# First layer's projections: bias columns copied on ScalarE, the last values' buffer placed apart from the accumulators, the second layer's gate sums spread later

## The chip, the cores and the metric

The kernel runs on one core of one Trainium2 chip. The metric is device time in microseconds (us), taken from the start to the end of one execution on that core. The engines of the core are named as the profile names them: PE is the matrix engine (PEld its weight loads), DVE is VectorE, ACT is ScalarE, POOL is GpSimd, SP issues most transfers (SPq is its queue). Each engine works through its own instructions in order and waits at an instruction until what it needs is there.

## The reference, cut to what matters

Two layers run over 256 context tokens and 1024 latent tokens of width 1024. The first layer is a windowed attention, the second a latent attention. Both start with a normalisation whose scale and shift come from a conditioning vector; a gate from the same vector weighs the layer's output.

```python
def adaln(cond, w, bias):
    m = jax.nn.silu(cond) @ w + bias
    return jnp.split(m, 3, axis=-1)          # shift, scale, gate
...
    hx = rms_norm(x, norm_g[i]) * (1.0 + scale_x[:, None]) + shift_x[:, None]
    hc = rms_norm(ctx, norm_g[i]) * (1.0 + scale_c) + shift_c
...
    q, k, v, g = jnp.split(h @ w_in, [A_WIDTH, A_WIDTH + A_KV_WIDTH, A_WIDTH + 2 * A_KV_WIDTH], axis=-1)
...
    x = x + gate_x[:, None] * yx
```

All values are float32. The conditioning product (a vector of 1024 by a 1024 x 3072 matrix, for two conditioning vectors and two layers) is the part called "sums" below; `h @ w_in` with its 2560 output columns is the part called "projections".

## The kernel before, in words

A float32 product is made of three matmuls, one line each (L126, L127, L128 in the helper `mm3`): both operands are split into a rounded high part and a rest, and high x high, low x high and high x low are added in one PSUM bank. The helper `split` makes the two parts: L121 casts the high part on ACT, L122 subtracts it on POOL or DVE.

The first layer's input projection is cut into ten blocks of 256 columns (`blocks`; number 0 is the values, 1, 6, 8 and 9 are gates, 7 is the keys, the others are queries). A block's weights come in four pieces of two 128-row chunks each (`Pieces`), loaded into float32 staging and cast into one of two weight buffers. A projection (`proj_t`, written below as block/group/half) takes one half of a block (128 columns) and one group of tokens: group 0 is the 256 context tokens, groups 1 and 2 are 512 latent tokens each. It consists of 24 matmuls into one of six PSUM banks that are used in turn (banks 0 to 5). The shift of the normalisation isn't added to the tokens: two more columns (256 and 257 of group 0) carry it through the same matmuls, so that the product's columns 256 and 257 are the bias of that half block, and are copied out of PSUM (L489). `post_t` empties the bank with that bias: L501 on ACT for a gate block (the result is stored by L502 on SP), L532 on ACT and L533 on DVE for queries of group 0, L507 on ACT followed by L508, L514, L529 on DVE (the rotation) for queries of groups 1 and 2, with stores L537 on SP.

The values (block 0) are computed first, without the shift, into five buffers `Vraw`, one per 256 tokens. Their bias comes later (`v_bias`): L446 and L455 on PE, L459 on DVE adds it to each of the five buffers, and `split` casts them (L121 on ACT, L122 on POOL).

The conditioning sums that the first attention doesn't need at once are worked off in small steps between the projections (`ada_rest`): a group is 512 of the 3072 columns, and each of its eight 128-row chunks is multiplied by a conditioning scalar and added to an accumulator on DVE (L191 the first chunk, L193 the others). A group has two accumulators (one per conditioning vector), the last two groups only one. After a group's last chunk PE sums over the partitions (L203, or L220 for a gate group), and DVE adds the bias (L211, or L221 for a gate). `ada_run(n)` takes n of these steps. The accumulators `acc1` lie at 30 and 32 KB of the float arena, the second of them also holds the small copy `mtmp` of `v_bias` until L455 has read it; a fifth `Vraw` buffer lies at 30 KB too.

All this is written as a program in order, but a scheduler places the instructions on each engine, by the data they need and its own estimates of when things are ready; what lies in one buffer is kept in order by waits. So an edit moves instructions on several engines, and their new order is shown below.

Of the kernel before, what the change touches and what calls it, by code (L numbers as in the profile page):

```python
# [34 lines left out]
class Ring:  # L35
# [6 lines left out]
    def next(self):  # L42
        b = self.bufs[self.i % len(self.bufs)]
        self.i += 1
        return b


def shp(ap, *dims):
    n = 1
    for d in dims:  # L50
        n *= d
    ap = ap[:, 0:n]
    if len(dims) == 1:
        return ap
    names = "abcdefg"[: len(dims)]
    kw = {c: d for c, d in zip(names[1:], dims[1:])}
    return ap.rearrange("p (" + " ".join(names) + ") -> p " + " ".join(names), **kw)
# [3 lines left out]
def kernel(ctx: ExitStack, tc: tile.TileContext, t, out, dbg=None):  # L61
    nc = tc.nc
# [23 lines left out]
    def r_at(kb, *dims):  # L86
        n = int(np.prod(dims))
        return shp(R[:, int(kb * KB) : int(kb * KB) + n], *dims)

    def f_at(kb, *dims):  # L90
        n = int(np.prod(dims))
        return shp(F[:, int(kb * KB) : int(kb * KB) + n], *dims)
# [31 lines left out]
    def mm3(o, a, b, first, last):  # L124
        (ah, al), (bh, bl) = a, b
        nc.tensor.matmul(o, ah, bh, start=first, stop=False)  # L126
        nc.tensor.matmul(o, al, bh, start=False, stop=False)  # L127
        nc.tensor.matmul(o, ah, bl, start=False, stop=last)  # L128
# [170 lines left out]
    wst = [80 + Z, 96 + Z]  # L299
    kT = r_at(112 + Z, 4, TOK)  # L300
    V = r_at(132 + Z, NT, 4, 128)
    Vraw = [f_at(o, 2, 256) for o in (0, 2, 10, 12, 30)]
    cosa = f_at(0, SEQ)
    sina = f_at(10, SEQ)
    stg = Ring(F, [4, 6, 8], 512)
# [76 lines left out]
    def ada_run(n):  # L382
        for _ in range(n):
            next(ada, None)
# [86 lines left out]
    bias = {}  # L471

    def proj_t(bi, gp, c):

        W = wt[bi]
        ps = pss()
        if gp:
            o = shp(ps, 2, 256)
            m = [hw[gp][:, :, s] for s in range(2)]
        else:  # L480
            o = ps[:, 0:258]
            m = [hT[0][:, s] for s in range(2)]
        cs = slice(c * 128, c * 128 + 128)
        for k in range(8):
            b = [x[:, :, k, :] if gp else x[:, k, :] for x in m]
            mm3(o, [W[:, s, k, cs] for s in range(2)], b, k == 0, k == 7)
        if gp == 0:
            bias[bi, c] = biases()
            nc.vector.tensor_copy(bias[bi, c], ps[:, 256:258])  # L489
        return ps  # L490

    def post_t(bi, gp, c, ps):
# [335 lines left out]
    for i, (gp, c) in enumerate([(1, 0), (1, 1), (2, 0), (2, 1)]):  # L828
        held.append((1, gp, c, proj_t(1, gp, c)))
        if i == 0:  # L830
            ada0.cols(0, 0, acc0[0], pst())
        if i == 1:
            ada0.cols(0, 1, acc0[1], pst())
            nc.scalar.copy(hT[0][:, 0, :, 256:258], ada0.B)
            nc.vector.tensor_sub(hT[0][:, 1, :, 256:258], ada0.B, hT[0][:, 0, :, 256:258].bitcast(F32))
            nc.vector.tensor_copy(B32[:, :, 0:2], ada0.B)
            vb = v_bias()
        if i == 2:
            next(vb)
        if i == 3:  # L840
            next(vb)
            load(out=cosa, in_=t["cos_a"])
            load(out=sina, in_=t["sin_a"])
            ada = ada_rest()
    for c in range(2):
        ps = proj_t(1, 0, c)
        for x in held[c::2]:
            post_t(*x)
        post_t(1, 0, c, ps)
        for _ in range(2):  # L850
            pieces.cast()
            pieces.load()
    for bi in range(2, 8):
        for i, (gp, c) in enumerate([(0, 0), (0, 1), (1, 0), (1, 1), (2, 0), (2, 1)]):
            post_t(bi, gp, c, proj_t(bi, gp, c))
            if bi < 7:
                ada_run(4 if gp == 0 else 6 if bi == 6 else 2)
            if 1 <= i < 5:
                pieces.cast()
                pieces.load()  # L860
    for bi in (8, 9):
        for c in range(2):
            ps = proj_t(bi, 0, c)
            if bi == 8:
                pieces.cast()
                pieces.load()
                pieces.cast()
            post_t(bi, 0, c, ps)
            ada_run(4)
    for gp in (1, 2):  # L870
        for bi in (8, 9):
            for c in range(2):
                if (bi, gp, c) == (8, 2, 0):
                    load2(out=mask, in_=t["mask"])
                    load2(out=gx, in_=gate_d[0, 0, :].partition_broadcast(128))
                    load2(out=gc, in_=gate_d[0, 1, :].partition_broadcast(128))
                    units[0].prep_q()
                    units[0].prep()
                    units[1].prep_q()
                if (bi, gp, c) == (9, 2, 0):  # L880
                    units[1].prep()
                    units[2].prep_q()
                    for h in range(4):
                        units[0].score(h)
                post_t(bi, gp, c, proj_t(bi, gp, c))
                ada_run(1)
                for _ in range(2 if gp == 2 else bi - 8):
                    next(wo_fill, None)

# [817 lines left out]
```

## Time and profile before

| | us |
|---|---|
| median of 3 runs | 1592.23 (1592.12 to 1593.79) |
| profiled execution, its own time | 1592.02 |
| its span | 1590.2 |
| PE busy in the span | 1544.0 |
| DVE, ACT, POOL busy | 994.1, 771.3, 750.1 |

The difference of 1.8 us between the profiled execution's time and its span lies around the span. The projections of the first layer run from about 95 to 355 us of the span. In most stages the matmuls follow each other without a gap, and so the time is read best from the few places where PE waits. A matmul's start to the next one's start is 0.12 us for 258 columns and 0.23 us for 512 at full clock.

### The profile page before, as it was taken

How to read it: one execution, taken by the hardware profiler on the slowest of the kernel's cores; microseconds unless marked ns; L12 is line 12 of the kernel's file. 1: busy time of each engine (PE TensorE's matmuls, PEld its weight loads, DVE VectorE, ACT ScalarE, POOL GpSimd, SP SyncE). 2: the span in 40 equal slices, each digit the busy share in tenths (PEclk: the TensorE clock that was granted, in tenths of full speed). 3: DMA queues.
4: the chain of work that ended last, by engine and by line, in shares of the span. 5: the costliest groups of instructions: out<-in, count | busy, mean ns of one | idle time of the engine just before them, and what ended most of it. 6: DMA issues, size and time to landing. Idle time of an engine off the chain costs nothing.

```text
span 1590.2 us, 26835 instructions
## 1 busy us (share of the span) xinstructions
PE 1544.0 (97%) x9830; PEld 1228.2 (77%) x9830; DVE 994.1 (63%) x1773; ACT 771.3 (49%) x1468; POOL 750.1 (47%) x805
## 2 busy tenths in 40 slices
PE   7989999998999999998999999999999999999998
PEld 3878888786878888887998899766766766766687
DVE  2867997827867777778525302666667566567354
ACT  3522222248767777767413332455555555545322
POOL 1241121125665444454214250488688688689410
PEclk8999999999999999999999999999999999999999
DMA  7456665544343333337103753313232323244251
GB/s 250 157 155 186 202 199 186 179 137 119 98 126 93 94 91 91 92 99 219 37 31 114 264 175 94 103 31 103 68 96 81 84 80 103 61 136 111 68 166 67
DMA packets 147204, 192.81 MB, mean 121 GB/s; under 512 B 13937, under 2 KB 84081, under 8 KB 147073
## 3 DMA queue, kind: packets, MB, share of 16 engines
q1 hardware_dynamic: 145456, 188.94, 40.0%
q10 hardware_dynamic: 1616, 2.17, 0.5%
q8 instruction: 77, 1.26, 0.3%
q14 instruction: 55, 0.44, 0.1%
HBM read 144.90 MB, written 46.15 MB: 120 GB/s over the span
## 4 chain that ended last, share of the span: by engine, by line
PE 84%; DVE 4%; POOL 4%; issue 3%; ACT 3%; DMA 2%; SPq 0%; POOLq 0%; ACTq 0%; DVEq 0%
PE PB L126 14%; PE PB L127 14%; PE PB L128 14%; PE PB L1334 11%; PE PB L1356 8%; PE PB L1297 4%; PE PB L616 4%; PE PB L657 4%; PE PB L647 4%; PE PB L1305 1%; DVE arena_f L193 1%; PE PB L1385 1%; ACT arena_r L121 1%; DVE arena_r L122 1%; POOL arena_r L122 1%
## 5 line engine op out<-in xcount | busy, mean ns | idle before, releaser
L126 PE MATMUL PB<-arena_r 128*128 128x512 f32 (+3 forms) x1496 | 509.6, 342 | 12.0 <-ACT arena_f L501 5.4
L127 PE MATMUL PB<-arena_r 128*128 128x512 f32 (+3 forms) x1496 | 503.6, 337 | 2.6 <-POOL arena_r L684 0.8
L128 PE MATMUL PB<-arena_r 128*128 128x512 f32 (+3 forms) x1496 | 502.0, 336 | 0.0
L1348 POOL TENSOR_TENSOR arena_f<-arena_f 128x512 f32<-128x512 f32 x252 | 325.0, 1290 | 79.4 <-ACT arena_f L1340 62.6
L126 PEld LDWEIGHTS PB<-arena_r 128*128 128x128 f32 x1496 | 285.1, 191 | 49.6 <-ACT arena_f L501 5.6
L127 PEld LDWEIGHTS PB<-arena_r 128*128 128x128 f32 x1496 | 286.3, 191 | 30.3 <-DVE arena_r L122 1.9
L128 PEld LDWEIGHTS PB<-arena_r 128*128 128x128 f32 x1496 | 286.2, 191 | 29.2 <-issue 1.7
L122 POOL TENSOR_TENSOR arena_r<-arena_f,arena_r 128x512 fp32r<-128x512 f32 x88 | 119.5, 1372 | 291.2 <-ACT arena_r L121 240.6
L1340 ACT ACTIVATE arena_f<-PB 128x1024 f32<-128x1024 f32 x160 | 164.3, 1027 | 108.4 <-PE PB L1334 68.4
L1299 DVE TENSOR_REDUCE arena_f<-PB 128x1 f32<-128x1024 f32 x128 | 156.0, 1219 | 86.6 <-PE PB L1297 86.5
L1334 PE MATMUL PB<-arena_r 64*128 64x512 f32 (+1 forms) x1600 | 202.2, 392 | 0.3 <-ACT arena_f L1340 0.3
L1334 PEld LDWEIGHTS PB<-arena_r 64*128 64x128 f32 (+1 forms) x1600 | 146.0, 185 | 31.5 <-ACT arena_f L1340 1.8
L122 DVE TENSOR_TENSOR arena_r<-PB,arena_r 128x512 fp32r<-128x512 f32 (+1 forms) x186 | 124.1, 674 | 62.2 <-ACT arena_r L121 61.2
L1356 PE MATMUL PB<-arena_f 128*64 128x512 f32 x640 | 144.4, 597 | 0.0
L627 DVE CUSTOM_DVE_ANT_0 arena_f<-PB,arena_f,small 128x640 f32<-128x640 f32 (+2 forms) x176 | 125.2, 722 | 19.5 <-PE PB L616 12.8
L630 ACT ACTIVATE arena_f<-arena_f,small 128x640 f32<-128x640 f32 (+2 forms) x160 | 119.5, 747 | 35.1 <-DVE small L627 32.5
L121 ACT CAST arena_r<-PB 128x512 fp32r<-128x512 f32 (+1 forms) x186 | 105.3, 573 | 46.9 <-PE PB L647 44.2
L121 ACT CAST arena_r<-arena_f 128x512 fp32r<-128x512 f32 (+3 forms) x141 | 83.7, 602 | 75.8 <-PE PB L127 11.8
L657 PE MATMUL PB<-arena_r 128*128 128x512 f32 x336 | 115.7, 428 | 0.5 <-DVE arena_f L669 0.4
L616 PE MATMUL PB<-arena_r 128*128 128x256 f32 (+1 forms) x576 | 111.0, 308 | 1.6 <-DVE small L627 1.3
L1356 PEld LDWEIGHTS PB<-arena_f 128*64 128x64 f32 x640 | 43.1, 136 | 83.2 <-issue 79.9
L647 PE MATMUL PB<-ident,arena_f 128*128 128x128 f32 x672 | 103.9, 274 | 1.3 <-DVE arena_r L122 1.1
(179 smaller groups left out, 1930.5 us busy)
## 6 DMA issues: line engine op xcount, KB each, us to landing
arena_f<-ada_w SPq DMA_DIRECT2D x47, 512.0 KB, 4.5
arena_r<-q_d SPq DMA_DIRECT2D x80, 256.0 KB, 4.1
arena_r<-qn_d SPq DMA_DIRECT2D x64, 256.0 KB, 3.8
arena_r<-qr_d SPq DMA_DIRECT2D x192, 64.0 KB, 3.2
arena_f<-a_w_in SPq DMA_DIRECT2D x40, 256.0 KB, 3.4
arena_f<-x SPq DMA_DIRECT2D x16, 512.0 KB, 4.4
g_d<-arena_f SPq DMA_DIRECT2D x32, 256.0 KB, 3.3
q_d<-arena_f SPq DMA_DIRECT2D x64, 128.0 KB, 2.7
```

The lines of the kernel that those rows point to most:

```text
L121: nc.scalar.copy(hi, src)
L122: (lo_eng or nc.vector).tensor_sub(lo, src, hi.bitcast(F32))
L126: nc.tensor.matmul(o, ah, bh, start=first, stop=False)
L127: nc.tensor.matmul(o, al, bh, start=False, stop=False)
L128: nc.tensor.matmul(o, ah, bl, start=False, stop=last)
L616: nc.tensor.matmul(S[:, at : at + n], qT[:, s, hq, :], kT[:, g, k : k + n], start=s == 0, stop=s == 1)
L647: nc.tensor.transpose(pt[:, h, :], self.Ps[h][:, ci * 128 : ci * 128 + 128], ident)
L657: nc.tensor.matmul(self.pv, V[:, self.chunks[ci], self.g, :], PT[:, s], start=ci == 0 and s == 0, stop=ci == self.m - 1 and s == 1,)
L1334: nc.tensor.matmul(S[:, t], k[r, c : c + 128], q[r], start=j == 0, stop=j == 4)
L1340: nc.scalar.activation(E, self.S, AF.Exp)
L1348: eng.tensor_add(self.acc, self.acc, E[:, t])
L1356: nc.tensor.matmul(self.pv[p : p + 64], Vq[:, cs[t], self.h % 4, :], E[:, t], start=i == 0, stop=i == 4)
```

## The change

Three edits, and what they do to the order of the instructions:

1. The two bias columns of each context projection are copied out of PSUM by ACT instead of DVE (18 instructions L489).
2. The fifth `Vraw` buffer moves from 30 KB to 34 KB of the float arena. At 34 KB lies also the first buffer of the ring `qst`, in which the queries of block 2 are prepared, and one buffer of the input ring `xr`.
3. The steps of the sums are spread otherwise in blocks 8 and 9: two instead of four after each context projection, three instead of one after each projection of group 1, none after group 2. The last 17 steps, the second layer's two gate groups, are the ones that move.

```diff
-    Vraw = [f_at(o, 2, 256) for o in (0, 2, 10, 12, 30)]
+    Vraw = [f_at(o, 2, 256) for o in (0, 2, 10, 12, 34)]
...
         if gp == 0:
             bias[bi, c] = biases()
-            nc.vector.tensor_copy(bias[bi, c], ps[:, 256:258])
+            nc.scalar.copy(bias[bi, c], ps[:, 256:258])
         return ps
...
             post_t(bi, 0, c, ps)
-            ada_run(4)
+            ada_run(2)
...
                 post_t(bi, gp, c, proj_t(bi, gp, c))
-                ada_run(1)
+                ada_run(3 if gp == 1 else 0)
```

**DVE where the values get their bias.** Before (L459 is the values' bias, L489 the copies of block 1's bias columns, L191 and L193 the first group of sums):

```order
L459 TENSOR_TENSOR arena_f<-arena_f,PB 128x512 [waits PE_49]
L459 TENSOR_TENSOR arena_f<-arena_f,PB 128x512 x4
L489 COPY small<-PB 128x2 [waits PE_49]
L191 TENSOR_SCALAR arena_f<-arena_f,small 128x512 [waits DMAHW3_49,Activation_49]
L193 SCALAR_TENSOR_TENSOR arena_f<-arena_f,small 128x512 [waits DVE_49]
L191 TENSOR_SCALAR arena_f<-arena_f,small 128x512 [waits Pool_49]
L193 SCALAR_TENSOR_TENSOR arena_f<-arena_f,small 128x512 [waits DMAHW4_49,DVE_49]
L193 SCALAR_TENSOR_TENSOR arena_f<-arena_f,small 128x512 [waits DVE_49]
L489 COPY small<-PB 128x2 [waits PE_49]
```

The second L191 waits for POOL, and the copy of the bias of projection 1/0/1 stands three sums behind it. With the change, at the same place:

```order
L836 COPY arena_f<-small 128x8x2
L193 SCALAR_TENSOR_TENSOR arena_f<-arena_f,small 128x512 [waits DMAHW4_49,DVE_49]
L193 SCALAR_TENSOR_TENSOR arena_f<-arena_f,small 128x512 [waits DVE_49]
L193 SCALAR_TENSOR_TENSOR arena_f<-arena_f,small 128x512 [waits DMAHW5_49,DVE_49]
L193 SCALAR_TENSOR_TENSOR arena_f<-arena_f,small 128x512 [waits DVE_49]
L193 SCALAR_TENSOR_TENSOR arena_f<-arena_f,small 128x512 [waits DMAHW6_49,DVE_49]
L193 SCALAR_TENSOR_TENSOR arena_f<-arena_f,small 128x512 [waits DVE_49]
L459 TENSOR_TENSOR arena_f<-arena_f,PB 128x512 [waits PE_49]
L459 TENSOR_TENSOR arena_f<-arena_f,PB 128x512 x4
L191 TENSOR_SCALAR arena_f<-arena_f,small 128x512 [waits Activation_49]
L193 SCALAR_TENSOR_TENSOR arena_f<-arena_f,small 128x512 [waits DVE_49] x7
L533 SCALAR_TENSOR_TENSOR arena_f<-PB,small,arena_f 128x256 [waits PE_49,Activation_49] x2
```

The copies and the wait for POOL are gone from DVE here. One accumulator's eight sums stand ahead of L459 (its first two just ahead of L836), the other's eight behind it.

**ACT at the same place.** Before (the first rows are the values' casts, L501 empties the banks of block 1):

```order
L121 CAST arena_r<-arena_f 128x8x64 [waits DVE_49] x4
L121 CAST arena_r<-arena_f 128x8x64 [waits DVE_49,Activation_49]
L501 ACTIVATE arena_f<-PB,small 128x512 [waits DVE_49]
L501 ACTIVATE arena_f<-PB,small 128x512
L501 ACTIVATE arena_f<-PB,small 128x256 [waits PE_49]
L121 CAST arena_r<-arena_f 128x512 [waits DMAHW1_49,PE_49,Pool_49]
L121 CAST arena_r<-arena_f 128x512 [waits DMAHW2_49,PE_49,Pool_49]
L121 CAST arena_r<-arena_f 128x512 [waits DMAHW3_49,PE_49,Pool_49]
L501 ACTIVATE arena_f<-PB,small 128x512 [waits DVE_49]
```

The last row is the one that empties bank 1 (projection 1/1/1); it waits for DVE's copy. With the change:

```order
L121 CAST arena_r<-arena_f 128x8x64 [waits DVE_49] x4
L489 COPY small<-PB 128x2 [waits PE_49]
L121 CAST arena_r<-arena_f 128x8x64 [waits DVE_49]
L501 ACTIVATE arena_f<-PB,small 128x512 [waits Activation_49]
L501 ACTIVATE arena_f<-PB,small 128x512
L501 ACTIVATE arena_f<-PB,small 128x256
L121 CAST arena_r<-arena_f 128x512 [waits DMAHW1_49,PE_49,Pool_49]
L489 COPY small<-PB 128x2 [waits PE_49]
L121 CAST arena_r<-arena_f 128x512 [waits DMAHW2_49,Pool_49]
L501 ACTIVATE arena_f<-PB,small 128x512 [waits Activation_49]
L121 CAST arena_r<-arena_f 128x512 [waits DMAHW3_49,Pool_49]
L501 ACTIVATE arena_f<-PB,small 128x512 [waits DMAHW6_49]
```

The tenth row empties bank 1 now: two copies have come in ahead of it, one piece's cast has gone behind it, and it waits for nothing outside ACT. Behind these rows, the first L532 of block 2 has taken over the wait for POOL (its buffer is the one at 34 KB).

**PE at the end of the sums.** Before (L220 is the partition sum of the second layer's first gate group; 128x258 rows are projection 9/0/1, the 128x512 rows 8/1/0):

```order
L127 MATMUL PB<-arena_r 128x258
L220 MATMUL PB<-arena_f,small 2x512 [waits DVE_49]
L128 MATMUL PB<-arena_r 128x258
L126 MATMUL PB<-arena_r 128x258
L127 MATMUL PB<-arena_r 128x258
L128 MATMUL PB<-arena_r 128x258
L126 MATMUL PB<-arena_r 128x512
L127 MATMUL PB<-arena_r 128x512
```

It stands four matmuls ahead of the end of projection 9/0/1. With the change:

```order
L126 MATMUL PB<-arena_r 128x512
L127 MATMUL PB<-arena_r 128x512
L128 MATMUL PB<-arena_r 128x512
L220 MATMUL PB<-arena_f,small 2x512 [waits DVE_49]
L126 MATMUL PB<-arena_r 128x512
L127 MATMUL PB<-arena_r 128x512
```

It stands behind the whole of projection 8/1/0 now, 28 matmuls later; the second gate group's L220 goes from behind 30 of the 48 matmuls of 8/1/0 and 8/1/1 to behind projection 9/1/0, 48 matmuls after the first one.

## The prediction

> **What bounds the kernel now.** I read the page first: PE is busy for nearly the whole span, and it carries most of the chain that ended last. So the time changes where PE waits or runs slowly, and hardly elsewhere.
>
> ```profile
> PE 1544.0 (97%) x9830; PEld 1228.2 (77%) x9830; DVE 994.1 (63%) x1773; ACT 771.3 (49%) x1468; POOL 750.1 (47%) x805
> PE 84%; DVE 4%; POOL 4%; issue 3%; ACT 3%; DMA 2%; SPq 0%; POOLq 0%; ACTq 0%; DVEq 0%
> ```
>
> Next the waits of PE alone, from 100 to 345 us, where all three edits lie (engine, line, whom it waited for: total, times, longest):
>
> ```profile
> PE PB L126 <- ACT arena_f L501: 5.4, 1, 5.4
> PE PB L220 <- DVE arena_f L193: 2.4, 2, 2.1
> ```
>
> There are only these three stops. The stage view shows what each costs, as PE busy (instructions), DVE, ACT, POOL and the granted clock:
>
> ```profile
> 100.35:109.87 9.52, 9.52 (x76) 9.21 (x75) 6.15 (x9) 6.11 (x11) 7.29 (x7) 1.00 0.37 103
> 109.87:115.29 5.42, 0.01 (x2) 0.00 (x1) 5.42 (x6) 0.74 (x2) 4.03 (x3) 0.80 0.56 206
> 115.29:120.00 4.71, 4.71 (x22) 4.71 (x23) 4.38 (x8) 1.36 (x3) 0.00 (x0) 0.51 0.73 227
> 120.00:283.00 163.00, 163.00 (x849) 138.08 (x849) 137.32 (x228) 43.43 (x75) 30.88 (x21) 1.00 0.63 187
> 302.30:304.50 2.20, 0.09 (x2) 0.03 (x2) 2.08 (x4) 0.98 (x2) 0.00 (x0) 0.94 0.92 322
> 304.50:307.50 3.00, 3.00 (x7) 1.29 (x8) 1.07 (x2) 0.18 (x1) 0.00 (x0) 0.50 1.06 398
> ```
>
> After both longer stops PE runs at half clock for a while (0.51, 0.50). In between it never stops in 163 us.
>
> The first stop, in order of time (start, duration, engine, line):
>
> ```profile
> 101.25 3.08 DVE L459 TENSOR_TENSOR arena_f<-arena_f,PB 128x512 f32<-128x512 f32 x5 [8.80 <-PE PB L455]
> 101.97 3.07 ACT L121 CAST arena_r<-arena_f 128x512 fp32r<-128x512 f32 x5 [2.90 <-DVE arena_f L459]
> 102.67 11.23 POOL L122 TENSOR_TENSOR arena_r<-arena_f,arena_r 128x512 fp32r<-128x512 f32 x8 [2.23 <-ACT arena_r L121]
> 104.94 1.63 ACT L501 ACTIVATE arena_f<-PB,small 128x512 f32<-128x512 f32 x3
> 106.45 1.66 ACT L121 CAST arena_r<-arena_f 128x512 fp32r<-128x512 f32 x3
> 109.59 0.28 PE L128 MATMUL PB<-arena_r 128*128 128x258 f32 x1
> 109.64 1.47 DVE L191 TENSOR_SCALAR arena_f<-arena_f,small 128x512 f32<-128x512 f32 x1 [2.44 <-POOL arena_r L122]
> 111.03 3.41 DVE L193 SCALAR_TENSOR_TENSOR arena_f<-arena_f,small 128x512 f32<-128x512 f32 x2
> 114.37 0.15 DVE L489 COPY small<-PB 128x2 f32<-128x2 f32 x1
> 114.55 1.63 ACT L501 ACTIVATE arena_f<-PB,small 128x512 f32<-128x512 f32 x3 [6.43 <-DVE small L489]
> 115.29 0.58 PE L126 MATMUL PB<-arena_r 128*128 128x258 f32 x1 [5.41 <-ACT arena_f L501]
> ```
>
> Read it upwards. PE wants bank 1 for projection 2/0/1; L501 on ACT must empty it, and lacks a bias that L489 copies on DVE in 0.15 us; DVE is kept by sums, the first of which (L191) waited 2.44 us for POOL's last read of the fifth value buffer.
>
> The second stop:
>
> ```profile
> 302.08 0.28 PE L127 MATMUL PB<-arena_r 128*128 128x258 f32 x1
> 304.47 1.87 PE L220 MATMUL PB<-arena_f,small 128*2 128x512 f32 x2 [2.11 <-DVE arena_f L193]
> 306.26 0.58 PE L128 MATMUL PB<-arena_r 128*128 128x258 f32 x1
> 307.70 0.39 PE L127 MATMUL PB<-arena_r 128*128 128x512 f32 x1
> 314.71 1.02 PE L220 MATMUL PB<-arena_f,small 128*2 128x512 f32 x2 [0.24 <-DVE arena_f L193]
> 315.66 0.50 PE L126 MATMUL PB<-arena_r 128*128 128x512 f32 x1
> ```
>
> PE reaches the gate's partition sum before DVE's last two L193 are done:
>
> ```profile
> 302.88 1.54 DVE L193 SCALAR_TENSOR_TENSOR arena_f<-arena_f,small 128x512 f32<-128x512 f32 x2
> ```
>
> **The change, part by part.** *First stop.* The buffer at 34 KB removes the wait of L191 for POOL, and the copy on ACT takes L489 from behind the sums. Either alone would take most of the stop; together nothing of DVE stands between PE and bank 1. What ACT must now do before it empties bank 1: five value casts, three L501, two piece casts and two copies. From 101.97 the five casts, three L501 and three casts before ended at 106.45 + 1.66 = 108.11. One cast fewer (0.55) and two copies more follow. The trace has no copy of two columns on ACT; the nearest row above is L532's 256 columns, the nearest below a cast of 16 columns:
>
> ```profile
> L532 ACT ACTIVATE arena_f<-PB,small 128x256 fp32r<-128x256 f32 x8 | 3.8, 474 | 13.4 <-DVE small L489 10.5 <-DMA q_d<-arena_f 2.9
> L834 ACT CAST arena_r<-small x1: 207/207/207, 92.0 to 92.0; 128x16 fp32r<-128x16 f32 x1
> ```
>
> Between 0.21 and 0.47 us each; I take 0.21, since two columns are nearer to 16 than to 256. Bank 1 is then free at 108.11 - 0.55 + 0.42 + 0.65 (an L501 of 512 columns; 1.63 is two of them and one of 256) = 108.6, at worst 109.2. PE wants it at 109.71 (the last start, 109.59, and 0.12, which a matmul of 258 columns takes from start to start: 9.52 us for 76). So the stop is gone, by a margin of 0.5 to 1.1 us. Its worth: 115.29 - 109.71 = 5.58 us, and the half clock behind it: 22 instructions in 4.71 us that take 22 x 0.12 = 2.64 at full clock, 2.07. Together 7.65 us.
>
> All 18 copies cost ACT 3.8 us (8.5 at the upper price), hidden in a stretch where ACT is busy 43 of 163 us and PE waits for nobody, with six banks between them. Without that cover the 3.8 us would be on the path.
>
> The wait for POOL isn't deleted but goes to the first L532 of block 2, with L501 of 1/0/1, the next copies and L507 of 2/1/0 queued behind it. POOL's fifth value subtraction ended by 109.64, when L191 was let go; L532 comes later than that in any case, so it costs nothing. What is late next on ACT is L501 of 1/2/1: it takes the first store's buffer again.
>
> ```profile
> 108.38 0.34 SPq L843 DMA_DIRECT2D arena_f<-sin_a  x1
> 108.84 6.74 SPq L502 DMA_DIRECT2D g_d<-arena_f  x4
> g_d<-arena_f SPq DMA_DIRECT2D x4, 256.0 KB, 4.7
> ```
>
> The stores stand on SP behind the rotation table, which itself waits for POOL's fourth value read; the first is issued at 108.84 and lands 4.7 us later, 113.5. ACT then empties bank 3 by 114.3. PE wants bank 3 at 109.71 + 2.9 (projection 2/0/1) + 5.4 (2/1/0) = 118.0: 3.7 us to spare.
>
> DVE's sums move into its idle 8.80 us ahead of L459, against POOL's pieces there, and a sum beside POOL takes up to 1.75 us instead of 0.75:
>
> ```profile
> 91.83 0.17 DVE L211 TENSOR_TENSOR small<-PB,small 128x8 f32<-128x8 f32 x1 [3.65 <-PE PB L203]
> L193 DVE SCALAR_TENSOR_TENSOR arena_f<-arena_f,small x19: 744/750/1745, 84.7 to 123.0; 128x512 f32<-128x512 f32 x19
> 94.39 3.78 POOL L122 TENSOR_TENSOR arena_r<-arena_f,arena_r 128x512 fp32r<-128x512 f32 x3 [33.48 <-PE PB L446]
> 99.14 1.29 POOL L122 TENSOR_TENSOR arena_r<-arena_f,arena_r 128x512 fp32r<-128x512 f32 x1 [0.98 <-ACT arena_r L121]
> ```
>
> L211 at 91.83, one sum and two small instructions of about 0.2 us come first, then six sums from about 93.1: two before POOL starts, then one per 1.7 us until 98.2, one in POOL's pause, the last by 100.8 at the latest. L459 isn't held up (101.25). The page "SBUF — State Buffer" of the Trainium skill, section "Who interferes with whom", says that a DVE instruction with two SBUF inputs and a GpSimd one lock each other out for a whole instruction; the trace agrees (1745 ns against 750), and this speaks against the new place of the sums.
>
> *Second stop.* L220 stands 28 matmuls later. DVE's chain there loses three copies and stays as it is; relative to PE it ends where it ended, at 304.4 on the old clock, while PE without the stop would arrive at 302.20 (302.08 and 0.12) + 0.48 + 24 x 0.223 = 308.0 (0.223 for 512 columns: 25.00 us for 112 in the stage from 316 to 341 below). The second gate group can start on DVE only after L221, then takes L191 and seven L193. At the 0.77 of an L193 (1.54 for two) for all nine that is 6.9 us, and PE has 48 x 0.223 = 10.7 us of other matmuls. Both stops go, with about 4 us to spare. Worth: 304.47 - 302.20 = 2.27; the pair of L220 1.79 from start to start against 0.95 for the second pair (315.66 - 314.71) or less, 0.84; then 306.26 to 307.70, 1.44 for five matmuls that take 0.71, 0.73; and the 0.24 of the second pair. Together 4.1 us.
>
> The half clock after a stop of only 2.1 us is seen here. The page "TensorE: Matmul & The Clock Gate" of the Trainium skill, section "Why this matters for your kernels", has the clock fall only after pauses over about 3 us. By that rule this stop would be worth 2.5 instead of 4.1 and the sum would be 10.2; the granted clock of 0.50 decides against it.
>
> *Downstream.* PE works without a stop to the end of the projections, so all of it arrives there:
>
> ```profile
> 316.00:341.00 25.00, 25.00 (x112) 20.70 (x111) 3.21 (x5) 7.53 (x12) 5.20 (x4) 1.00 0.42 133
> 341.00:360.00 19.00, 19.00 (x107) 16.36 (x105) 8.76 (x37) 13.03 (x24) 4.65 (x7) 1.00 0.60 176
> 360.00:400.00 40.00, 35.79 (x210) 27.55 (x209) 31.59 (x93) 33.28 (x94) 23.31 (x43) 1.00 0.40 107
> ```
>
> The attention's beginning (360 to 400) is a mix of PE, ACT and DVE with DMA at 0.40, each started by PE's results, so it should move as a whole.
>
> **Sum:** 7.65 + 4.1 = 11.7 us. The profiled execution, 1592.02, becomes 1580.3; the median shown is 0.2 above it: 1580.5.
>
> **The rivals.**
>
> *A, one stop returns.* The new orders have margins of 0.5 to 1.1 us at bank 1. If six sums at 1.75 us all collide with POOL, they end at 93.1 + 10.5 = 103.6, L459 is 2.3 us late, bank 1 is free at 110.9 and PE stops for 1.2 us, with up to 2.1 us of half clock behind it: gain 8.4, time 1583.8. If instead the second stop returns whole, the gain is 7.65 and the time 1584.6. Against: POOL works 5 of these 8 us only, and the margins at L220 are 4 us. Chance 0.17.
>
> *B, the gain is given back.* PE comes 11.7 us earlier to the first attention scores, and what they need (weights of the output projection, stored queries) is set by transfers. Then the time stays at about 1592. For: PE is idle 4.2 us of 360 to 400. Against: DMA at 0.40 there, and the loads are issued when PE has freed their buffers, so they move too. Chance 0.07.
>
> *C, slower.* ACT's queue, in which L501 of 1/2/1 now waits for the first store's landing with the copies behind it, becomes what PE waits for at bank 3. It costs PE from a landing at 117.3 on, one for one and 2.1 more for the clock; from 18 us after the issue (11.7 - 2.1 = 9.6 us beyond 117.3) the kernel is slower than before, at 20 us by some 1.9 us, at 25 us by 7 (1599). Against: 4.7 us measured. With whatever else turns all of it round, chance 0.04.
>
> **How the numbers follow.** The forecast has 0.72, A 0.17, B 0.07, C 0.04. A measurement of this kernel tells about 0.2% (3.2 us) from no change, so forecast and A count as faster: 0.89; B is no change, C slower. The forecast's own bounds: the copies' price moves nothing while the margin holds; the half clock may end earlier or start elsewhere (2 us either way), so 1578 at the low end. The high end takes in A and part of a return downstream: 1587.
>
> **What would show it right or wrong.** Right: no stop of PE at L126 near 110 us; granted clock 1.00 from 100 to 300; both L220 pairs without idle time ahead of them; the first scores (L616) some 11.7 us earlier; the rest of the trace the same, moved. Wrong: L126 waiting again for L501 near 110 or at 118 (A, C); L459 starting later than 101.5 (A); the scores early but the end not (B).

## The result, and the profile after

| | before | after |
|---|---|---|
| median of 6 runs, us | 1592.17 (1591.27 to 1593.79) | 1582.12 (1581.13 to 1583.18) |
| profiled execution, us | 1592.02 | 1581.13 |
| its span, us | 1590.2 | 1579.3 |

The ratio is 0.9936 (95% interval 0.9924 to 0.9949): 10.05 us less by the medians, 10.9 by the two profiled executions. The prediction had 11.7 less and the time 1580.5, with a range of 1578 to 1587.

The waits of PE in the changed kernel, in the window that holds all three edits (80 to 345 us; engine, line, whom it waited for: total, times, longest). One short stop is left, and it is neither of the two that were forecast to go:

```profile
PE PB L203 <- DVE arena_f L193: 0.3, 1, 0.3
```

The stage view of the changed kernel (PE, PEld, DVE, ACT, POOL busy, then the granted clock, the DMA share and GB/s):

```profile
100.00:120.00 20.00, 20.00 (x135) 18.57 (x134) 17.32 (x16) 9.91 (x22) 15.10 (x10) 1.00 0.61 191
120.00:283.00 163.00, 162.59 (x844) 137.34 (x843) 136.88 (x218) 45.54 (x88) 33.46 (x23) 1.00 0.64 185
302.00:340.00 38.00, 38.00 (x170) 29.74 (x169) 13.18 (x30) 13.24 (x25) 6.63 (x7) 1.00 0.65 190
```

PE is busy for the whole of 100 to 120 and of 302 to 340, at a granted clock of 1.00, where it stood still for 5.4 and 2.4 us before. In between 0.41 us of 163 is missing, which it wasn't before.

The place of the first stop in the changed kernel, in order of time:

```profile
94.10 7.43 DVE L193 SCALAR_TENSOR_TENSOR arena_f<-arena_f,small 128x512 f32<-128x512 f32 x6
102.61 3.08 DVE L459 TENSOR_TENSOR arena_f<-arena_f,PB 128x512 f32<-128x512 f32 x5 [1.08 <-PE PB L455]
105.65 0.15 ACT L489 COPY small<-PB 128x2 f32<-128x2 f32 x1
105.72 0.62 ACT L121 CAST arena_r<-arena_f 128x512 fp32r<-128x512 f32 x1
106.90 10.96 DVE L193 SCALAR_TENSOR_TENSOR arena_f<-arena_f,small 128x512 f32<-128x512 f32 x7
108.38 0.16 ACT L489 COPY small<-PB 128x2 f32<-128x2 f32 x1
108.97 0.69 ACT L501 ACTIVATE arena_f<-PB,small 128x512 f32<-128x512 f32 x1
114.98 0.69 ACT L501 ACTIVATE arena_f<-PB,small 128x512 f32<-128x512 f32 x1 [4.82 <-DMA g_d<-arena_f]
```

DVE's six sums end at 101.53, ahead of L459, which waits for PE alone (1.08 us). Its next seven sums take 10.96 us beside POOL, 1.57 each instead of 0.75, but nobody's bias stands behind them: the copy is on ACT, and L501 empties bank 1 from 108.97 to 109.66. L501 of projection 1/2/1 waits 4.82 us for the first store to land and ends at 115.67, as it was forecast to.

The place of the second stop in the changed kernel, on DVE:

```profile
293.23 6.55 DVE L193 SCALAR_TENSOR_TENSOR arena_f<-arena_f,small 128x512 f32<-128x512 f32 x7
303.79 0.68 DVE L221 TENSOR_TENSOR arena_f<-PB,arena_f 2x512 f32<-2x512 f32 x1 [3.40 <-PE PB L220]
304.89 5.48 DVE L193 SCALAR_TENSOR_TENSOR arena_f<-arena_f,small 128x512 f32<-128x512 f32 x7
315.84 0.68 DVE L221 TENSOR_TENSOR arena_f<-PB,arena_f 2x512 f32<-2x512 f32 x1 [5.47 <-PE PB L220]
```

The roles are exchanged: it is now DVE that waits for PE's sums (3.40 and 5.47 us), where PE waited for DVE.

For where the time went, the view of two lines by their first and last start: L455 (ahead of the first edit's effect) and L616 (the first attention scores, behind the last one). Before:

```profile
L455 PE MATMUL PB<-arena_f,small x4: 377/378/379, 100.2 to 100.8; 128*128 128x256 f32 x4
L616 PE MATMUL PB<-arena_r x576: 274/283/425, 341.6 to 698.9; 128*128 128x256 f32 x130, 128*128 128x384 f32 x62
```

and after:

```profile
L455 PE MATMUL PB<-arena_f,small x4: 378/378/379, 101.5 to 102.2; 128*128 128x256 f32 x4
L616 PE MATMUL PB<-arena_r x576: 274/283/425, 332.2 to 689.5; 128*128 128x256 f32 x130, 128*128 128x384 f32 x62
```

From L455 to L616 it is 241.4 us before and 230.7 after: 10.7 us gained in the stage that the edits touch. Ahead of it 1.3 us is lost (101.5 against 100.2), behind it 1.5 is gained (1248.6 against 1247.1 us to the end of the span): together the 10.9 us of the spans. Whether the 1.3 and 1.5 belong to the change is one of the questions of the runs below.

### The profile page after: what moved, and what is told of

Read it like the earlier page. It is cut to its first block, busy times and chain, and to the rows that moved or that the text cites. A ratio compares the mean times of both kernels' runs of the same rounds, so it can differ in the third digit from the quotient of the medians.

```text
span 1579.3 us, 26829 instructions
## 1 busy us (share of the span) xinstructions
PE 1542.5 (98%) x9830; PEld 1227.4 (78%) x9830; DVE 998.0 (63%) x1755; ACT 772.2 (49%) x1486; POOL 751.9 (48%) x805
## 4 chain that ended last, share of the span: by engine, by line
PE 73%; DVE 7%; issue 4%; POOL 3%; ACT 2%; DMA 2%; SPq 0%; ACTq 0%; DVEq 0%; POOLq 0%
PE PB L1334 12%; PE PB L126 11%; PE PB L127 11%; PE PB L128 11%; PE PB L1356 9%; PE PB L1297 4%; PE PB L616 4%; PE PB L657 4%; PE PB L647 4%; DVE arena_f L193 2%; DVE arena_f L514 1%; PE PB L1305 1%; ACT arena_r L121 1%; PE PB L1385 1%; PE PB L676 1%
## 5 line engine op out<-in xcount | busy, mean ns | idle before, releaser
L616 PE MATMUL PB<-arena_r 128*128 128x256 f32 (+1 forms) x576 | 111.1, 308 | 1.5 <-DVE small L627 1.3
```

The source lines that it names most:

```text
L616: nc.tensor.matmul(S[:, at : at + n], qT[:, s, hq, :], kT[:, g, k : k + n], start=s == 0, stop=s == 1)
```

## The experiments

The theory is that of the prediction: two stops of PE, each with its own causes, and a stage that keeps what it gains. What it leaves to be told apart: whether buffer and copies do the same thing twice, whether the two stops add, and where the last microsecond went. The first four kernels ran together, with a median of 1592.87 for the kernel before (1589.82 to 1595.17, 16 runs). For all kernels the same three pieces of the span, from the first starts of L455 and L616 and the span:

| kernel | to L455 | L455 to L616 | L616 to the end | span |
|---|---|---|---|---|
| before | 100.2 | 241.4 | 1248.6 | 1590.2 |
| changed | 101.5 | 230.7 | 1247.1 | 1579.3 |
| buffer alone | 101.2 | 237.7 | 1247.5 | 1586.4 |
| copies alone | 101.8 | 233.9 | 1249.7 | 1585.4 |
| buffer and copies | 100.5 | 233.4 | 1248.3 | 1582.2 |
| spread alone | 101.0 | 237.5 | 1247.4 | 1585.9 |
| changed, and block 6 | 100.4 | 229.8 | 1247.9 | 1578.1 |
| changed, again | 101.9 | 229.8 | 1248.3 | 1580.0 |

The first column varies by 1.7 us and the third by 2.6, with no order by edit; so only the second tells edits apart, and to about a microsecond: each row is one execution, and the changed kernel, the only one profiled twice, differs from itself by 0.9 there.

### Buffer alone

```diff
-    Vraw = [f_at(o, 2, 256) for o in (0, 2, 10, 12, 30)]
+    Vraw = [f_at(o, 2, 256) for o in (0, 2, 10, 12, 34)]
```

> Only the fifth value buffer moves to 34 KB. My theory: both causes of the first stop stand in DVE's queue, the wait for POOL and the sums ahead of the copy of 1/0/1's bias. With the buffer moved, eight sums go ahead of the values' bias, the wait for POOL is gone, but an L191 and three L193 still stand ahead of the second L489, beside POOL at up to 1.7 us each. They end near 110.7, PE gets bank 1 near 111.7 and stops for about 2 us (before 5.4), with up to 2 us of half clock behind it. The second stop (2.1 us at L220) stays. Time 1586.5 to 1588.5, gain 3.7 to 5.7. Rival (the buffer alone was the cause): no stop at 110 us, gain 7 to 8, about 1585.

Measured: 1589.08 us (10 runs), ratio 0.9978 (0.9968 to 0.9988), the stage 3.7 us shorter. PE's waits in this kernel:

```profile
PE PB L220 <- DVE arena_f L193: 3.0, 2, 2.1
PE PB L126 <- ACT arena_f L501: 1.6, 1, 1.6
PE PB L203 <- DVE arena_f L193: 0.9, 2, 0.6
```

and why the first stop isn't gone, on DVE and ACT:

```profile
106.59 5.06 DVE L193 SCALAR_TENSOR_TENSOR arena_f<-arena_f,small 128x512 f32<-128x512 f32 x3
111.57 0.15 DVE L489 COPY small<-PB 128x2 f32<-128x2 f32 x1
111.75 0.69 ACT L501 ACTIVATE arena_f<-PB,small 128x512 f32<-128x512 f32 x1 [3.16 <-DVE small L489]
```

The wait of L191 for POOL has gone, but the copy of 0.15 us still stands behind three sums that take 1.7 us each, and L501 waits 3.16 us for it. 1.6 of the 5.4 us remain. The time is a little above what the theory expected. Two things came up that the prediction doesn't have: a stop at L203, longer than in the changed kernel, and half clock behind it. The stage view behind the first stop, and around L203:

```profile
112.00:114.00 2.00, 1.51 (x12) 1.51 (x13) 1.96 (x2) 1.00 (x3) 2.00 (x2) 1.00 0.93 360
244.14:247.55 3.41, 2.54 (x20) 2.16 (x18) 1.82 (x4) 0.69 (x1) 0.00 (x0) 1.00 0.78 219
247.55:250.96 3.41, 3.41 (x10) 2.64 (x9) 3.41 (x8) 0.00 (x0) 0.00 (x0) 0.50 0.78 261
```

Behind the 1.6 us the granted clock stays at 1.00. Behind L203's it falls to 0.50 for 3.41 us, which loses 3.41 x 0.50 = 1.7 us. With the 0.9 us of the stop itself, 2.6 us are lost there, against 3.8 us less waiting and 2.07 less half clock at the first stop: 3.3 by this count, 3.7 measured. The count leaves out L220, where PE waits 0.6 us longer than before (3.0 against 2.4) and no half clock follows (1.6 us less, see below); with both it gives 4.3, so such a count is good to about half a microsecond.

### Copies alone

```diff
-            nc.vector.tensor_copy(bias[bi, c], ps[:, 256:258])
+            nc.scalar.copy(bias[bi, c], ps[:, 256:258])
```

> Only the copies go to ACT. My theory: PE no longer waits for anything of DVE at bank 1, no stop near 110 us, 7.7 us earlier from there. DVE however still holds all 16 sums of the first group behind the values' bias and the wait for POOL, so it comes to block 2 some 4 us later than with the whole change; if DVE's chain through blocks 2 to 6 is nearly as long as PE's (in the whole change PE stopped at the column sums L203 near 243 us for DVE), PE now stops there for longer, 2 to 4 us, and the gain is 4 to 6: 1586 to 1588. Rival (DVE has slack there, the buffer is not needed once the copies are on ACT): gain 6.8 to 7.7, 1584.5 to 1585.4.

Measured: 1587.19 us (5 runs), ratio 0.9966 (0.9954 to 0.9979), the stage 7.5 us shorter. PE's waits:

```profile
PE PB L220 <- DVE arena_f L193: 2.7, 2, 2.0
PE PB L203 <- DVE arena_f L193: 0.8, 2, 0.5
```

The first stop is gone entirely, with L191 still waiting for POOL and the accumulators where they were. So that wait matters only through the copy behind it. The kernel's time is the one that the theory expected (a gain of 4 to 6 us; 5.7 by the medians), but partly by luck: the theory had a stop of 2 to 4 us at L203, and it is 0.8. The stage, 7.5 us shorter, lies where the rival had the gain (6.8 to 7.7), and the profiled execution loses 1.6 us against the kernel before ahead of the stage and 1.1 behind it. The stage's 7.5 doesn't decide for the rival either, since no half clock follows here, neither behind L203 nor behind the 2.0 us at L220; how many of its executions have it isn't known.

### Buffer and copies, sums spread as before

> Both edits at the first stop, the sums spread as before. My theory (two separate stops that add): no stop near 110 us, a short one at L203 near 243 us (about 0.9 us with what it costs), the stop at L220 near 297 us stays at 2 us and more. Gain 6.8, time 1585.4. Rival (the sums' spread matters for the first part too, or the second stop vanishes by itself since DVE has fewer copies): gain 10, about 1582.

The edit is the two above together. Measured: 1583.96 us (5 runs), ratio 0.9946 (0.9932 to 0.996), the stage 8.0 us shorter. One wait of PE is left, and the stage view from it on:

```profile
PE PB L220 <- DVE arena_f L193: 2.0, 1, 2.0
```

```profile
294.20:297.61 3.41, 1.38 (x8) 0.52 (x6) 2.51 (x4) 0.45 (x1) 0.00 (x0) 1.00 0.96 323
297.61:301.02 3.41, 3.41 (x11) 2.67 (x11) 2.58 (x4) 1.15 (x3) 1.08 (x1) 0.50 1.06 403
301.02:304.00 2.98, 2.98 (x15) 2.42 (x14) 2.87 (x4) 0.00 (x0) 0.32 (x1) 1.00 0.69 212
```

The first stop is gone, and in this execution L203 doesn't stop PE. That it is the buffer which keeps DVE ahead there isn't shown: the changed kernel has buffer and copies too, and stops there in one execution of two (below). The second stop stays, with half clock behind it as before. The stage is only 0.5 us shorter than with the copies alone, but it holds 3.41 us at half clock, which cost 1.7 us, and that one holds none.

### Spread alone

```diff
-            ada_run(4)
+            ada_run(2)
...
-                ada_run(1)
+                ada_run(3 if gp == 1 else 0)
```

> Only the sums are spread later. My theory: the stop of 5.4 us near 110 us stays as it was, both stops at L220 go; gain 3.9 to 4.1, time 1588.2. Rival (the second stop is only moved to the later L220, where DVE's second gate group is late): gain under 2, above 1590.

Measured: 1589.82 us (7 runs), ratio 0.9973 (0.9962 to 0.9984), the stage 3.9 us shorter. PE's waits:

```profile
PE PB L126 <- ACT arena_f L501: 5.4, 1, 5.4
```

The first stop is whole and the second gone. The stage's two parts, 8.0 with buffer and copies and 3.9 with the spread, make 11.9; the whole change has 10.7 in one execution and 11.6 in another (below). They add, to within a microsecond. By the median this kernel is 1.6 us slower than the theory expected, though in the profiled execution (1587.72) the stage is as short as it had it; where the slower executions lose isn't known. The kernel with buffer and copies is 1.4 us faster than expected, and one part of that is that it doesn't stop at L203.

### The changed kernel with another spread in block 6, and the changed kernel again

Of the changed kernel's own loss the candidate was the stop at L203. The next kernel gives DVE more time there: of block 6's sums four instead of six are taken after each projection of group 1, and eight instead of six after each of group 2, which puts that L203 one projection later on PE and leaves the order on DVE, ACT and POOL.

```diff
-                ada_run(4 if gp == 0 else 6 if bi == 6 else 2)
+                ada_run(4 if gp == 0 else 2 if bi < 6 else 4 if gp == 1 else 8)
```

> The whole change, and in block 6 four sums instead of six after each projection of group 1 and eight instead of six after each of group 2. On PE only the column sum L203 near 243 us moves, one projection (24 matmuls, 5.4 us) later; DVE, ACT and POOL keep their order. My theory (DVE's chain reaches this L203 just as PE does, so what PE gained at the first stop is partly lost there: 0.3 us of waiting before the first two matmuls, 0.28 ahead of the other fourteen, with the restart 0.8 in all): no stop at L203, the stretch from the values' bias sum (L455) to the first scores (L616) 0.8 us shorter than in the changed kernel of the same call, and nothing else. Time 0.8 us below the changed kernel's, which one comparison of medians can hardly tell. Rival (DVE is the bound there, and PE only waits elsewhere): the stop moves to the next L203 or to the rotation's banks, and the stretch is as long as before.

> The changed kernel once more, beside the former one. My theory: ahead of the edits (up to L455) executions differ by 1.4 us, as the clock falls to half behind a stop of 1.04 us at 38 us or not, whatever the kernel; behind the projections by about 1 us more. So the ratio lies between 0.993 and 0.995, and the stretch from L455 to L616 takes 230.5 to 231.0 us, against 241.4 before. Rival (the gain is of the edits' place only in the first profile): the stretch differs by more than 1 us from 230.7.

Measured together, beside 1592.0 us for the kernel before: 1580.01 us (1579.25 to 1582.4, 5 runs), ratio 0.9927 (0.9914 to 0.9939) with block 6, and 1582.25 us (1579.26 to 1582.81, 5 runs), ratio 0.9932 (0.9919 to 0.9946) for the changed kernel again. In the first PE has no wait at all from 80 to 345 us, and DVE is done well before PE comes:

```profile
232.13 9.36 DVE L193 SCALAR_TENSOR_TENSOR arena_f<-arena_f,small 128x512 f32<-128x512 f32 x14
246.99 1.84 PE L203 MATMUL PB<-small,arena_f 128*128 128x2 f32 x16
```

The sums end at 241.5, PE wants them at 246.99. But the changed kernel, profiled again, has no wait there either, and the same stage, 229.8 us. So the two can't be told apart in the stage: the 0.8 us that were expected of block 6 are not found, and the expectation for the second run of the changed kernel, a stage of 230.5 to 231.0, missed too, by 0.7. The 2.2 us between their medians is more than the L203 stop can explain, and the intervals overlap. That the version with block 6 is better than the changed kernel is not shown.

What the second profile of the changed kernel does show is where the L203 stop comes from. In the first execution (rows on ACT, DVE and PE):

```profile
208.29 0.48 ACT L532 ACTIVATE arena_f<-PB,small 128x256 fp32r<-128x256 f32 x1 [4.71 <-DMA q_d<-arena_f]
208.81 0.48 DVE L533 SCALAR_TENSOR_TENSOR arena_f<-PB,small,arena_f 128x256 fp32r<-128x256 f32 x1 [0.69 <-ACT arena_f L532]
234.25 9.36 DVE L193 SCALAR_TENSOR_TENSOR arena_f<-arena_f,small 128x512 f32<-128x512 f32 x14
242.47 0.39 PE L128 MATMUL PB<-arena_r 128*128 128x512 f32 x1
243.00 0.38 PE L203 MATMUL PB<-small,arena_f 128*128 128x2 f32 x2
243.66 1.72 PE L203 MATMUL PB<-small,arena_f 128*128 128x2 f32 x14 [0.28 <-DVE arena_f L193]
245.24 0.48 PE L126 MATMUL PB<-arena_r 128*128 128x512 f32 x1
```

and in the second:

```profile
206.62 0.48 ACT L532 ACTIVATE arena_f<-PB,small 128x256 fp32r<-128x256 f32 x1 [3.10 <-DMA q_d<-arena_f]
207.97 0.48 DVE L533 SCALAR_TENSOR_TENSOR arena_f<-PB,small,arena_f 128x256 fp32r<-128x256 f32 x1
233.39 9.36 DVE L193 SCALAR_TENSOR_TENSOR arena_f<-arena_f,small 128x512 f32<-128x512 f32 x14
243.01 1.84 PE L203 MATMUL PB<-small,arena_f 128*128 128x2 f32 x16
244.71 0.49 PE L126 MATMUL PB<-arena_r 128*128 128x512 f32 x1
```

PE is ready for L203 at 242.70 in the first (242.47 and the 0.23 of a matmul of 512 columns) and at 243.01 in the second. In the first L532, which waits for a store of queries to leave its buffer, starts 1.67 us later, L533 on DVE waits 0.69 us for it, and DVE's sums start 0.86 later and end at 243.61 instead of 242.75. So in the first the first two matmuls start 0.30 us late, which the view of waits doesn't list, and the others wait 0.28. From PE's being ready to the next projection's first matmul it is 2.54 us in the first and 1.70 in the second: the stop costs 0.8 us, and that is nearly all of the 0.9 by which the stage differs. In the kernel before, the same place reads

```profile
240.82 8.03 DVE L193 SCALAR_TENSOR_TENSOR arena_f<-arena_f,small 128x512 f32<-128x512 f32 x12
249.02 1.84 PE L203 MATMUL PB<-small,arena_f 128*128 128x2 f32 x16
```

where the sums end at 248.85 and PE comes at 249.02: no wait is shown, and 0.17 us is all that keeps it away.

## Why the prediction was right, and where it wasn't

**First stop, 7.65 us: right.** Buffer and copies together shorten the stage by 8.0 us. Each step of the working is found: the six sums ahead of L459, forecast to end by 100.8 at the latest, end at 101.53 in an execution that runs 1.3 us later; L459 isn't held up; bank 1 is free at 109.66 (forecast 108.6, with the 1.3 109.9) for a PE that wants it at 109.71 + 1.3 = 111.0; bank 3 is free 4.82 us of waiting later, at 115.67, against a use at 118.0 + 1.3. The copy's price was oversized: 0.15 to 0.16 us as a duration, and 0.07 from its start to the next one's start (105.65 to 105.72), where 0.21 was taken.

**"Either alone would take most of the stop": right.** The copies alone take all of it. The buffer alone takes 3.8 of 5.4 us; it frees L191 but not the copy, which still stands behind three sums beside POOL, 5.06 us.

**Second stop, 4.1 us: right in size, weaker in its ground.** The spread alone brings 3.9 us, and PE comes to L220 3.40 and 5.47 us after DVE is done, where about 4 were forecast. 1.6 of the 4.1 was the half clock behind a stop of 2.1 us, which the prediction read off one execution (granted 0.50). In the run with buffer and copies it comes again (0.50 for 3.41 us). In the runs with buffer alone and copies alone L220 stops PE for 2.11 and 2.03 us, and no half clock follows. Here is the buffer alone, PE's row and then the stage view around it:

```profile
302.58 1.02 PE L220 MATMUL PB<-arena_f,small 128*2 128x512 f32 x2 [2.11 <-DVE arena_f L193]
```

```profile
298.75:302.16 3.41, 1.72 (x15) 1.51 (x13) 3.30 (x6) 0.98 (x2) 0.00 (x0) 1.00 0.64 198
302.16:305.58 3.42, 3.00 (x13) 1.87 (x14) 2.14 (x5) 1.10 (x2) 0.68 (x1) 1.00 1.05 397
```

So the stop's price is 2.5 or 4.1 us, by execution, and the prediction should have carried both. The kernel before was profiled once, and that execution had the dear one. That the stage's gain came so near to the forecast is in part luck of that execution.

**"In between it never stops in 163 us": true of the profile, and the step that failed.** It was read as a cover for everything that DVE does there. Two of the kernels with a part of the change, and one execution of two of the whole, stop at L203, for 0.3 to 0.9 us by the view of waits and up to 1.7 more of half clock. The sums were due 0.17 us before PE came, and the wait view shows only waits that happened. This is the term that the sum lacked: 0.8 us in the profiled execution, most of what lies between the 10.7 gained in its stage and the 11.6 of the other.

**Downstream: right.** From L616 to the end the eight profiles lie between 1247.1 and 1249.7 us. The gain arrives; the 1.5 us more in the profiled execution lies within that spread.

**The rivals.** A (a stop returns at bank 1 or at L220) and C (PE waits at bank 3) didn't come: the wait view names L203 alone. Nor did B: from the first scores to the end takes no longer than before. A had the right kind of event in the wrong place.

**The signs.** L459 starts at 102.61, later than the 101.5 that was named as a sign of A, and the scores come 9.4 us earlier, not 11.7. Both hold the 1.3 us that this execution lost ahead of the stage: L459 starts 1.1 us after L455's first start in both kernels.

**The sum.** 11.7 was forecast for the stage, and 10.7 and 11.6 were measured. The span's 10.9 holds 1.3 us lost at the start and 1.5 gained at the end, both within what the eight profiles differ by there: the start is explained below, the end isn't. Of the 1.65 us between 11.7 and the 10.05 of the medians, the L203 stop can account for about 0.8 in the executions that have it, and against executions of the kernel before without the half clock behind L220, if there are any, the gain is 1.6 smaller; how it divides between these, starts and ends stays open.

## What to carry to other kernels

A tiny instruction in an in-order queue costs what stands ahead of it: 0.15 us of copy behind a few sums set a PSUM bank free 5.6 us late, and moving the copy to another engine was worth more than removing a wait ahead of it. Two stops of the engine that bounds the kernel add when the work between them has slack; so look for the hand-overs where the producer ends just before the consumer comes (0.17 us here), since the views of waits don't list them and an edit that shifts one engine against another turns them into stops. What lies outside the stage that the edits touch varied by 1.7 us ahead of it and 2.6 behind it over the eight profiles, so compare the stage, between two lines, before the span.

## What the runs showed of the hardware

Half clock doesn't follow from the length of a stop alone. It came behind stops of 5.4 us (both), behind 2.0 and 2.1 us in two profiles and not in two others, behind the 0.6 and 0.3 us of L203 with the buffer alone, and not behind 1.6 us in the same execution.

What the length leaves out is where the stop lies. Each stretch of half clock in the stage is 3.41 us long (the rows from 247.55 with the buffer alone and from 297.61 with buffer and copies) or twice that (behind the 5.4 us). In the kernel before, the first such steps behind its two stops are

```profile
113.11:116.52 3.41, 1.23 (x5) 1.23 (x6) 3.41 (x6) 1.63 (x3) 0.79 (x1) 0.50 0.17 64
304.25:307.66 3.41, 3.19 (x7) 1.45 (x8) 1.37 (x5) 0.34 (x1) 0.00 (x0) 0.50 1.05 397
```

with 1.00 in the 3.41 us ahead of each; they start 191.14 us apart, 56 times 3.41. So in these rows the clock changes on a grid of 3.41 us, and a stop of 2 us falls into one step of it or over two. In the step ahead of the change PE is busy 1.38 of 3.41 us with buffer and copies, and half clock follows; with the buffer alone it is 1.72, and none follows. No share of busy time divides all cases, though: ahead of the half clock behind L203 it is 2.54 of 3.41 us, with 16 matmuls of two columns among 20. What counts as idle there stays open.

Half clock also explains the start. At 38 us each kernel has the same stop of PE, here from the waits of the kernel before:

```profile
PE PB L126 <- ACT arena_r L419: 1.0, 1, 1.0
```

The stretch behind it reads in the kernel before

```profile
39.60:42.50 2.90, 2.90 (x27) 2.90 (x27) 2.12 (x6) 1.98 (x5) 0.00 (x0) 1.00 0.42 95
```

and in the changed kernel

```profile
39.60:42.50 2.90, 2.90 (x15) 2.90 (x15) 1.21 (x4) 0.56 (x2) 0.00 (x0) 0.50 0.11 39
```

Twelve instructions fewer of 0.12 us are 1.4 us, about the start's difference of 1.3. Four of the eight profiles have it (the changed kernel in both, the buffer and the copies alone), four don't, the one with block 6 among them, whose code is the changed kernel's up to there.

The page "TensorE: Matmul & The Clock Gate" of the Trainium skill, section "What's actually happening", says that the clock falls after an idle window of about 3.4 us and that the window runs freely, wherever the kernel stands in it. That the same stop is followed by half clock in one execution and not in the next, and the steps of 3.41 us, agree with a window that runs freely; that PE is busy 1.38 and 2.54 of the 3.41 us ahead of half clock doesn't agree with a whole window of idleness, and the granted 0.50 behind them decides.
